# Start of a one-core conv and attention trunk: modulation maps loaded first in a ring, later modulation on half maps

## The chip, the core and the metric

One core of a Trainium2 chip runs the whole program. Its engines are PE (TensorE, matrix multiplies), DVE (VectorE), ACT (ScalarE), POOL (GpSimd) and SP (SyncE, which here only issues transfers). Each engine works through its own list of instructions in order, and waits at an instruction until what it needs is there. The metric is the device time of one execution in microseconds; lower is better.

## What is computed

The reference is a stack of two layers over 1024 latent tokens and 256 context tokens with 1024 features. Layer 0 mixes tokens by a Conformer convolution, layer 1 by attention; both are followed by a SwiGLU network. Every sub-layer is normalized, scaled and shifted by values that come from the conditioning vectors through one linear map per layer:

```python
mod_x = (silu_c @ w_mod[i] + b_mod[i])[:, None, :]
mod_c = silu_cc @ w_mod[i] + b_mod[i]
sh_x, sc_x, g_x, shf_x, scf_x, gf_x = jnp.split(mod_x, N_MOD, axis=-1)
hx = rmsnorm(x, norm_g[i, 0]) * (1.0 + sc_x) + sh_x
hc = rmsnorm(ctx, norm_g[i, 0]) * (1.0 + sc_c) + sh_c
# convolution module of layer 0, on hx and on hc
u = h @ w_pw1 + b_pw1
a, gt = jnp.split(u, 2, axis=-1)
u = a * jax.nn.sigmoid(gt)
u = depthwise_conv(u, w_dw, width=31) + b_dw
u = jax.nn.silu(layernorm(u, ln_g, ln_b))
return u @ w_pw2 + b_pw2
```

So `hx` and `hc` need the first two of the six parts of the modulation (shift and scale), and the rest is needed only behind the convolution.

## The kernel before

Features lie on partitions, in 8 groups of 128; tokens lie along the free dimension, in three pieces: C (256 context tokens), L (the first 512 latent ones) and R (the last 512). Products are made of three matmuls each: a 32-bit operand is split into a rounded part and a remainder (`wh` and `wl` for weights). A weight block of 128x1024 is loaded by SP into one of two buffers `wr`, rounded by ACT (L142), and its remainder is taken by DVE (L146) or POOL (L148).

The beginning, in `build`, has two stages.

In the first, the modulation map is cut into 48 maps of 128 columns (512 KB each). The first 16 (shift and scale) are multiplied on PE by `mod_pe` (L238), two for each of 8 feature groups `k`; their tiles `T_113`, `T_114` and `KB` form a ring of ten buffers. The loop over `k` also moves on the normalizations of C, L and R (`norm_in`): squares on ACT (L383, L386), their sum on DVE (L387), the sum over partitions on PE (L363), the inverse root in small steps on DVE (L368 and L329 to L337), its spread over partitions on PE (L375), and then for each `k` scale on DVE (L395), rounded part on ACT (L400) and remainder on DVE (L401). The rows of C, L and R are loaded by `load_x` into `HR`, `T_106` and `HS`; `cond_row` loads the conditioning vectors as rows (1 MB) for use by DVE.

In the second, `pw1` makes the first projection, block by block (`k` = 0 to 7), each over C, L and R; L457 is its last write for each piece. Copies of its result to the convolution's layout, `split_u` (L157), convolution maps built on DVE (L500, from the tap weights `craw`), convolution matmuls (L526 to L529) and the sum of their halves (L532, L552) run beside it, one convolution step at two of three turns. At each of these turns `modg` may also move on: it is `mod_dve`, which makes maps 16 to 39 of the modulation on DVE, two reductions of 128x1024 for each map (L268), from full maps loaded by SP, one into a tile of `KB` and the next into a weight buffer `wr`, in turn.

What stands where in each engine's list is decided when the program is built: a scheduler takes instructions by the order in which the code issues them, but lets one go ahead where it reckons that its engine would stand idle. Transfers go to the queue of the engine that issues them.

Of the kernel before, what the change touches and what calls it, by code (L numbers as in the profile page):

```python
# [15 lines left out]
P = 128  # L16
# [38 lines left out]
class Kern:  # L55
# [173 lines left out]
    def mod_pe(self, f, raw=None, rows=None):  # L229

        nc = self.nc
        out = self.bank("md")
        if raw is None:
            raw = self.raw()
        nc.sync.dma_start(raw, self.a["wmod"][f])
        with self.later(20):
            for k in range(KT):
                nc.tensor.matmul(out[0:2, 0:P], lhsT=self.cs[:, k, :], rhs=raw[:, k * P:(k + 1) * P],  # L238
                                 start=k == 0, stop=k == KT - 1)
        rows = self.sm(P) if rows is None else rows  # L240
        nc.scalar.copy(rows[0:2, :], out[0:2, 0:P])
        with self.later(40):
            nc.tensor.transpose(out[:, P:P + 2], rows[0:2, :], self.c["ident"][0:2, 0:2])
        for s in range(2):
            nc.scalar.activation(self.mod[0][s][:, f:f + 1], out[:, P + s:P + s + 1], AF.Identity,
                                 bias=self.c["bmod"][:, 0, f:f + 1], scale=1.0)
# [4 lines left out]

    def mod_dve(self, fs, cr, raws, junk):

        nc = self.nc

        def load(i):
            if i >= len(fs):
                return None
            raw = raws[i % len(raws)]
            if raw is None:  # L260
                raw = self.raw()
            nc.sync.dma_start(raw, self.a["wmodT"][0, fs[i]])
            return raw
        nxt = load(0)
        for i, f in enumerate(fs):
            raw, nxt = nxt, load(i + 1)
            for s in range(2):
                nc.vector.tensor_tensor_reduce(out=junk, in0=raw, in1=cr[:, s, :], scale=1.0, scalar=0.0,  # L268
                                               op0=ALU.mult, op1=ALU.add,
                                               accum_out=self.mod[0][s][:, f:f + 1])  # L270
                yield 1.13
        for s in range(2):
            m = self.mod[0][s][:, fs[0]:fs[-1] + 1]
            nc.vector.tensor_tensor(m, m, self.c["bmod"][:, 0, fs[0]:fs[-1] + 1], op=ALU.add)
# [670 lines left out]
    def build(self):  # L945
# [22 lines left out]
        raws = [raws[i][:, j] for j in range(4) for i in range(3) if j < raws[i].shape[1]]  # L968
        for k in range(KT):
            if k == 5:  # L970
                self.pre += [self.wload(a["pw1"][0]), self.wload(a["pw1"][KT])]
            self.mod_pe(k, raws[2 * k % len(raws)])
            self.mod_pe(8 + k, raws[(2 * k + 1) % len(raws)])
# [6 lines left out]
            if k == 1:  # L980
                load_x("L")
                self.cond_row(cr)
                for _ in range(KT + 1):
                    next(gL)
                next(gC)
            if k:
                next(gC)
                next(gL)
            if k == 3:
                xs["R"] = self.T("HS", [P, KT, 512])  # L990
                load_x("R")
                gR = self.norm_in(0, None, (None, "T4", "T5"), *PIECES["R"], hs["R"], xt=xs["R"])
            if k > 3:
                for _ in range(2):
# [24 lines left out]
        modg = self.mod_dve(range(16, 40), cr, (mraw, None), self.ps[:, 5:7].rearrange("p a b -> p (a b)"))  # L1019
# [3 lines left out]
        for k in range(KT):  # L1023
            for i, _ in enumerate(self.pw1(k, hs)):
# [7 lines left out]
                if i % 3 != 2:  # L1032
# [4 lines left out]
        for g0 in (0, CG // 2):  # L1037
            self.split_u(KT - 1, g0, g0 + CG // 2)
        self.derive(0, (1, 2))
# [293 lines left out]
```

## Time and profile before

| | |
|---|---|
| time of three runs | 3049.22, 3055.4, 3057.86 us; median 3055.4 |
| the profiled execution | 3058.17 us, span of its trace 3056.4 us |
| busy share of the span | PE 96%, DVE 62%, ACT 40%, POOL 9% |
| mean granted clock of PE | 0.974 of full speed |

The span runs from the first to the last instruction of the trace; the profiled execution's own time is 1.8 us longer. Shares over the whole span average stages with different limits, so what matters for the beginning is read from windows and from the order of instructions in time.

### The profile page before, as it was taken

Reading aid. Unit: us, or ns where it says so; the run is one execution under the profiler, and the core shown is the slowest. Engines: PE = TensorE matmul, PEld = TensorE weight load, DVE = VectorE, ACT = ScalarE, POOL = GpSimd, SP = SyncE. Lnnn points to the kernel's source line nnn. Section 1 sums busy time; section 2 is a strip of 40 time slices with the busy share of each in tenths; the row PEclk is TensorE's granted clock in tenths of the full one; section 3 lists DMA queues with packets and bytes.
Section 4 is the critical chain, followed back from the end, with each engine's and each line's share of the span. In section 5 each row is a group of like instructions: output and inputs, shape, how many; then the busy total and the mean of one; then the engine's idle time right before and its main releaser. Section 6 shows DMA issues by size and latency. Waiting matters only on the chain. (4 is left out here: it accounts for less than half of the span.)

```text
span 3056.4 us, 39302 instructions
## 1 busy us (share of the span) xinstructions
PE 2927.2 (96%) x15086; PEld 2438.8 (80%) x15086; DVE 1902.2 (62%) x3341; ACT 1207.4 (40%) x1981; POOL 261.1 (9%) x413
## 2 busy tenths in 40 slices
PE   7899969999999999999988999999999999999997
PEld 5788868888888888888877777777787778788886
DVE  5886777866566358333565899766666654743335
ACT  5222255432222234222333688645555542332222
POOL 0000000101112011000013111110000000100000
PEclk9999979999999999999989999989999999999999
DMA  6542424433346235333346311223223132443332
GB/s 236 147 122 75 122 76 138 159 114 126 119 156 198 67 105 157 105 97 97 126 134 151 88 45 47 92 70 90 72 69 86 58 135 95 148 136 97 97 93 66
DMA packets 140716, 336.96 MB, mean 110 GB/s; under 512 B 39920, under 2 KB 61424, under 8 KB 139376
## 3 DMA queue, kind: packets, MB, share of 16 engines
q1 hardware_dynamic: 76432, 221.94, 22.6%
q0 software_dynamic: 37984, 104.42, 11.5%
q10 hardware_dynamic: 26112, 8.10, 1.1%
q8 instruction: 118, 1.93, 0.3%
q14 instruction: 70, 0.57, 0.1%
HBM read 289.76 MB, written 39.19 MB: 108 GB/s over the span
## 5 line engine op out<-in xcount | busy, mean ns | idle before, releaser
L167 PE MATMUL ps<-T,wl 128*128 128x512 f32 (+1 forms) x2128 | 802.9, 378 | 11.8 <-DVE wl L146 11.8
L165 PE MATMUL ps<-T,wh 128*128 128x512 f32 (+1 forms) x2128 | 806.3, 380 | 6.9 <-ACT T L154 4.1
L166 PE MATMUL ps<-T,wh 128*128 128x512 f32 (+1 forms) x2064 | 777.9, 377 | 0.7 <-DVE T L157 0.7
L142 ACT CAST wh<-wr 128x1024 fp32r<-128x1024 f32 x296 | 310.8, 1050 | 796.8 <-PE ps L166 569.0
L146 DVE TENSOR_TENSOR wl<-wr,wh 128x1024 fp32r<-128x1024 f32 x288 | 352.0, 1223 | 311.5 <-ACT wh L142 307.1
L167 PEld LDWEIGHTS ps<-T,wl 128*128 128x128 f32 x2128 | 407.3, 192 | 85.9 <-DVE wl L146 14.1
L165 PEld LDWEIGHTS ps<-T,wh 128*128 128x128 f32 x2128 | 407.2, 192 | 79.7 <-ACT T L154 5.6
L166 PEld LDWEIGHTS ps<-T,wh 128*128 128x128 f32 x2064 | 395.5, 192 | 68.9 <-DVE T L157 2.0
L166 PE MATMUL ps<-HS,wh 128*128 128x512 f32 (+1 forms) x784 | 303.8, 388 | 0.0
L892 DVE TENSOR_TENSOR T<-ps,T 128x512 fp32r<-128x512 f32 x320 | 216.7, 686 | 110.9 <-ACT T L891 109.7
L167 PE MATMUL ps<-HS,wl 128*128 128x512 f32 (+1 forms) x720 | 278.9, 388 | 0.0
L165 PE MATMUL ps<-HS,wh 128*128 128x512 f32 (+1 forms) x720 | 278.7, 389 | 0.0
L891 ACT CAST T<-ps 128x512 fp32r<-128x512 f32 x320 | 185.9, 585 | 194.8 <-PE ps L888 172.8
L888 PE MATMUL ps<-cst,T 128*128 128x128 f32 x1100 | 192.2, 276 | 1.9 <-DVE T L892 1.8
L876 DVE TENSOR_SCALAR_CACHE_REDUCE T<-ps,rq 128x1280 f32<-128x1280 f32 x110 | 169.9, 1544 | 27.8 <-PE ps L870 23.0
L722 DVE TENSOR_TENSOR T<-ps,T 128x512 f32<-128x512 f32 (+1 forms) x168 | 110.3, 662 | 113.1 <-PE ps L167 112.2
L888 PEld LDWEIGHTS ps<-cst,T 128*128 128x128 f32 x1100 | 134.0, 142 | 49.0 <-DVE T L892 28.6
L878 ACT ACTIVATE T<-T,mn 128x1280 f32<-128x1280 f32 x110 | 150.4, 1367 | 57.1 <-DVE T L876 55.2
L166 PEld LDWEIGHTS ps<-HS,wh 128*128 128x128 f32 x784 | 147.5, 188 | 28.6 <-DVE HS L157 0.2
L697 DVE TENSOR_TENSOR sm<-sm,ps 128x256 f32<-128x256 f32 (+1 forms) x88 | 54.5, 619 | 181.4 <-PE ps L167 181.2
L870 PE MATMUL ps<-KB,q 128*128 128x512 f32 (+1 forms) x576 | 146.8, 374 | 14.2 <-DVE HS L876 9.9
L167 PEld LDWEIGHTS ps<-HS,wl 128*128 128x128 f32 x720 | 135.4, 188 | 27.0
(227 smaller groups left out, 4574.0 us busy)
## 6 DMA issues: line engine op xcount, KB each, us to landing
wr<-in_w SPq DMA_DIRECT2D x220, 512.0 KB, 3.5
q<-in_w SPq DMA_DIRECT2D x44, 512.0 KB, 3.5
wr<-in_pw SPq DMA_DIRECT2D x40, 512.0 KB, 3.6
HR<-in_wmodT POOLq DMA_DIRECT2D x56, 256.0 KB, 3.9
q<-in_wmodT POOLq DMA_DIRECT2D x56, 256.0 KB, 3.9
qsd<-T POOLq DMA_DIRECT2D x32, 256.0 KB, 10.7
q<-qsd POOLq DMA_DIRECT2D x32, 256.0 KB, 3.3
wr<-in_wo SPq DMA_DIRECT2D x16, 512.0 KB, 4.4
```

Of the source, the lines that this page charges most:

```text
L142: nc.scalar.copy(hi, raw)
L146: nc.vector.tensor_tensor(lo, raw, hi.bitcast(F32), op=ALU.subtract)
L165: nc.tensor.matmul(out[:, :n], lhsT=wh, rhs=xh, start=k == 0, stop=False)
L166: nc.tensor.matmul(out[:, :n], lhsT=wh, rhs=xl, start=False, stop=False)
L167: nc.tensor.matmul(out[:, :n], lhsT=wl, rhs=xh, start=False, stop=k == nk - 1)
L722: nc.vector.tensor_tensor(yd, out[:, :c1 - c0], yd, op=ALU.add)
L870: nc.tensor.matmul(sc[:, k0:k0 + w], lhsT=q[:, h, :], rhs=kt[:, p * TOK + k0:p * TOK + k0 + w], start=p == 0, stop=p == 1)
L876: nc.vector.tensor_scalar(out=pt, in0=sc, scalar1=rq[:, h:h + 1], scalar2=None, op0=ALU.mult, op1=ALU.min, accum_out=mn)
L878: nc.scalar.activation(pt, pt, AF.Exp, bias=mn, scale=-1.0, accum_out=sums[:, 0, h:h + 1])
L888: nc.tensor.transpose(tp[:, h * P:(h + 1) * P], Ps[h][:, j * P:(j + 1) * P], c["ident"])
L891: nc.scalar.copy(ph, tp)
L892: nc.vector.tensor_tensor(pl, tp, ph.bitcast(F32), op=ALU.subtract)
```

## The change

The first stage loads ahead: ten maps go out before the loop, six of them ahead of L's rows and four behind, and each further map is loaded into a ring buffer when that is free. R's rows are issued at `k` = 3, behind the first two weight blocks of the projection, and the conditioning rows behind R's rows. All weight remainders of the beginning are taken by DVE (`lo_dve`). In the second stage maps 16 to 39 are made by `mod_half`, which stood in the kernel already for later modulation: half maps (128x512) loaded by POOL into three buffers of their own, 96 reductions in place of 48, with a partial sum added at the end. The load of the first tap weights is tied behind R's last remainder by a copy of one column.

```diff
--- before.py
+++ after.py
@@ -226,13 +226,10 @@
         self.col = [[{} for s in range(2)] for l in range(2)]
 
 
-    def mod_pe(self, f, raw=None, rows=None):
+    def mod_pe(self, f, raw, rows=None):
 
         nc = self.nc
         out = self.bank("md")
-        if raw is None:
-            raw = self.raw()
-        nc.sync.dma_start(raw, self.a["wmod"][f])
         with self.later(20):
             for k in range(KT):
                 nc.tensor.matmul(out[0:2, 0:P], lhsT=self.cs[:, k, :], rhs=raw[:, k * P:(k + 1) * P],
@@ -248,30 +245,6 @@
     def cond_row(self, cr):
         self.nc.sync.dma_start(cr.rearrange("p s d -> p (s d)"), self.a["crow"].to_broadcast([P, 2048]))
         self.nc.scalar.activation(cr, cr, AF.Silu)
-
-    def mod_dve(self, fs, cr, raws, junk):
-
-        nc = self.nc
-
-        def load(i):
-            if i >= len(fs):
-                return None
-            raw = raws[i % len(raws)]
-            if raw is None:
-                raw = self.raw()
-            nc.sync.dma_start(raw, self.a["wmodT"][0, fs[i]])
-            return raw
-        nxt = load(0)
-        for i, f in enumerate(fs):
-            raw, nxt = nxt, load(i + 1)
-            for s in range(2):
-                nc.vector.tensor_tensor_reduce(out=junk, in0=raw, in1=cr[:, s, :], scale=1.0, scalar=0.0,
-                                               op0=ALU.mult, op1=ALU.add,
-                                               accum_out=self.mod[0][s][:, f:f + 1])
-                yield 1.13
-        for s in range(2):
-            m = self.mod[0][s][:, fs[0]:fs[-1] + 1]
-            nc.vector.tensor_tensor(m, m, self.c["bmod"][:, 0, fs[0]:fs[-1] + 1], op=ALU.add)
 
     def mod_half(self, l, fs, cr, raws, junk):
 
@@ -966,32 +939,39 @@
             col[("sh", 0)] = self.mod[0][s][:, 0:8]
         raws = [self.T(t, [P, 4, 1024]) for t in ("T4", "T5")] + [self.T("KB", [P, 2, 1024])]
         raws = [raws[i][:, j] for j in range(4) for i in range(3) if j < raws[i].shape[1]]
+
+        def load_map(i):
+            if i < 2 * KT:
+                nc.sync.dma_start(raws[i % len(raws)], a["wmod"][i % 2 * KT + i // 2])
+        for i in range(len(raws)):
+            if i == 6:
+                load_x("L")
+            load_map(i)
+        self.lo_dve = 1.0
         for k in range(KT):
-            if k == 5:
-                self.pre += [self.wload(a["pw1"][0]), self.wload(a["pw1"][KT])]
-            self.mod_pe(k, raws[2 * k % len(raws)])
-            self.mod_pe(8 + k, raws[(2 * k + 1) % len(raws)])
+            for i in (2 * k, 2 * k + 1):
+                self.mod_pe(i % 2 * KT + k, raws[i % len(raws)])
+                load_map(i + len(raws))
             for s in range(2):
                 nc.vector.scalar_tensor_tensor(out=self.col[0][s][0][:, k:k + 1], in0=self.mod[0][s][:, 8 + k:9 + k],
                                                scalar=1.0, in1=c["ng"][:, 0, 0, k:k + 1], op0=ALU.add, op1=ALU.mult)
             if k == 0:
                 for _ in range(KT + 1):
                     next(gC)
-            if k == 1:
-                load_x("L")
-                self.cond_row(cr)
+            if k == 2:
                 for _ in range(KT + 1):
                     next(gL)
-                next(gC)
-            if k:
-                next(gC)
+            next(gC)
+            if k >= 2:
                 next(gL)
             if k == 3:
+                self.pre += [self.wload(a["pw1"][0]), self.wload(a["pw1"][KT])]
                 xs["R"] = self.T("HS", [P, KT, 512])
                 load_x("R")
                 gR = self.norm_in(0, None, (None, "T4", "T5"), *PIECES["R"], hs["R"], xt=xs["R"])
+                self.cond_row(cr)
             if k > 3:
-                for _ in range(2):
+                for _ in range(3 if k < 6 else 2):
                     next(gR)
         for g in (gC, gL, gR):
             for _ in g:
@@ -1016,7 +996,9 @@
         self.cwq, self.cwi = [], 0
         for o, n in ((0, 2), (2 + NC_, 2), (UW - 2, 2)):
             nc.gpsimd.memset(self.U[:, :, o:o + n], 0.0)
-        modg = self.mod_dve(range(16, 40), cr, (mraw, None), self.ps[:, 5:7].rearrange("p a b -> p (a b)"))
+        raws = [mraw[:, :512], mraw[:, 512:], self.sp.tile([P, 512], F32, tag="mr", name="mr", bufs=1)]
+        modg = self.mod_half(0, range(16, 40), cr, raws, self.ps[:, 5, :])
+        nc.vector.tensor_copy(self.craw[:, 0:1], hs["R"][0][1][:, KT - 1, 0:1].bitcast(F32))
         nc.sync.dma_start(self.craw, a["wwin"][0])
         self.conv_maps()
         cg = self.conv()
@@ -1029,13 +1011,15 @@
                     self.more_maps([(cw[:, 2 * j], cw[:, 2 * j + 1]) for j in range(3)])
                 if 12 * k + i >= 22 and i % 3 != 1:
                     next(cg)
-                if i % 3 != 2:
+                for _ in range((1 + (i % 6 == 0)) if k else 0):
                     next(modg, None)
         nc.scalar.activation(self.tiny([P, 16], "nv")[:, :1], c["ones"], AF.Silu)
         for _ in range(4):
             next(cg)
         for g0 in (0, CG // 2):
             self.split_u(KT - 1, g0, g0 + CG // 2)
+        for _ in modg:
+            pass
         self.derive(0, (1, 2))
         for i, _ in enumerate(cg):
             if i in (2, 4):
```

`mod_half`, as it stands in both kernels (`self.tie` is not set yet at this place):

```python
        ahead = len(raws) - 1
        for i in range(ahead):
            load(i)
        for i in range(2 * len(fs)):
            f, h = fs[i // 2], i % 2
            load(i + ahead)
            for s in range(1 if l and f >= 16 else 2):
                nc.vector.tensor_tensor_reduce(out=junk, in0=raws[i % len(raws)], in1=cr[:, s, h * 512:h * 512 + 512],
                                               scale=1.0, scalar=0.0, op0=ALU.mult, op1=ALU.add,
                                               accum_out=(part[:, s] if h else self.mod[l][s])[:, f:f + 1])
                yield 1.0
```

First place: SP's queue from the issue of R's rows on (`HS<-in_xT`). `in_wmod` are maps for PE, `in_wmodT` maps for DVE, `in_pw1` weight blocks, `in_crow` the conditioning rows, `in_wwin` tap weights. Before:

```order
L958 DMA HS_365<-in_xT 128x2x512 x4
L235 DMA T4_113<-in_wmod 128x1024
L235 DMA T5_114<-in_wmod 128x1024
L141 DMA wr1_74<-in_pw1 128x1024
L141 DMA wr0_73<-in_pw1 128x1024
L235 DMA T4_113<-in_wmod 128x1024
L235 DMA T5_114<-in_wmod 128x1024
L235 DMA KB_115<-in_wmod 128x1024
L235 DMA T4_113<-in_wmod 128x1024
L235 DMA T5_114<-in_wmod 128x1024
L235 DMA KB_115<-in_wmod 128x1024
L262 DMA wr1_74<-in_wmodT 128x1024
```

In the changed kernel, from the fifteenth map on:

```order
L945 DMA T5_114<-in_wmod 128x1024
L945 DMA KB_115<-in_wmod 128x1024
L141 DMA wr1_74<-in_pw1 128x1024
L141 DMA wr0_73<-in_pw1 128x1024
L931 DMA HS_377<-in_xT 128x2x512 x4
L246 DMA HR_105<-in_crow 128x2048
L141 DMA wr1_74<-in_pw1 128x1024
L141 DMA wr0_73<-in_pw1 128x1024
L141 DMA wr1_74<-in_pw1 128x1024
L439 DMA KB_619<-HR_105 128x1x32 x4
L1002 DMA KB_619<-in_wwin 128x320
L141 DMA wr0_73<-in_pw1 128x1024
```

R's rows moved behind all maps and two weight blocks, the conditioning rows behind them; no map for DVE stands in this queue any more, and the tap weights stand in front of a weight block.

Second place: DVE at the end of R's inverse root (`nr`, `nq`, `nh`) and the first of R's applies (`sb<-HS`). L500 (before) builds convolution maps `T6`. Before:

```order
L337 SCALAR_TENSOR_TENSOR nr_565<-nq_567,nr_565 128x4
L500 TENSOR_TENSOR T6_621<-q_620,cst_75 128x640
L335 TENSOR_TENSOR nq_567<-nr_565 128x4
L500 TENSOR_TENSOR T6_621<-q_620,cst_75 128x640
L336 TENSOR_TENSOR nq_567<-nq_567,nh_566 128x4
L500 TENSOR_TENSOR T6_621<-q_620,cst_75 128x640
L337 SCALAR_TENSOR_TENSOR nr_565<-nq_567,nr_565 128x4
L335 TENSOR_TENSOR nq_567<-nr_565 128x4
L336 TENSOR_TENSOR nq_567<-nq_567,nh_566 128x4
L337 SCALAR_TENSOR_TENSOR nr_565<-nq_567,nr_565 128x4
L395 SCALAR_TENSOR_TENSOR sb_586<-HS_365,col000_111,ps_72 128x512
L395 SCALAR_TENSOR_TENSOR sb_590<-HS_365,col000_111,ps_72 128x512
```

In the changed kernel, where L430 is the projection's write, L368 and L374 scale and remainder, `T6_106` and `T3` piece L, `HS` and `T5` piece R:

```order
L310 SCALAR_TENSOR_TENSOR nr_557<-nq_559,nr_557 128x4
L430 SCALAR_TENSOR_TENSOR HR_105<-ps_72,cst_75,sm_681 128x256
L368 SCALAR_TENSOR_TENSOR sb_578<-HS_377,col000_111,ps_72 128x512
L368 SCALAR_TENSOR_TENSOR sb_582<-T6_106,col000_111,ps_72 128x512
L368 SCALAR_TENSOR_TENSOR sb_586<-T6_106,col000_111,ps_72 128x512
L374 SCALAR_TENSOR_TENSOR T5_577<-sb_578,mod00_101,T4_576 128x512
L374 SCALAR_TENSOR_TENSOR T3_326<-sb_582,mod00_101,T2_325 128x512
L368 SCALAR_TENSOR_TENSOR sb_590<-HS_377,col000_111,ps_72 128x512
L374 SCALAR_TENSOR_TENSOR T3_326<-sb_586,mod00_101,T2_325 128x512
L368 SCALAR_TENSOR_TENSOR sb_594<-HS_377,col000_111,ps_72 128x512
L374 SCALAR_TENSOR_TENSOR T5_577<-sb_590,mod00_101,T4_576 128x512
L368 SCALAR_TENSOR_TENSOR sb_598<-HS_377,col000_111,ps_72 128x512
```

Convolution maps left this place, and the last applies of piece L and a write of the projection came into it.

Third place: DVE early in block 2, behind the first sums of convolution halves (L532 before, L505 now). Reductions of the modulation are `ISA` rows with `mod00`, `mod01` (streams) or `mpart` (partial sums) as output, each followed by the read of its sum. Before:

```order
L500 TENSOR_TENSOR T6_621<-q_620,cst_75 128x640 x2
L532 TENSOR_TENSOR HR_105<-HR_105,ps_72 128x162
L268 ISA ps_72,mod01_102<-wr0_73,HR_105 128x1024
L268 ISA mod01_102 128x1
L268 ISA ps_72,mod00_101<-KB_619,HR_105 128x1024
L268 ISA mod00_101 128x1
L268 ISA ps_72,mod01_102<-KB_619,HR_105 128x1024
L268 ISA mod01_102 128x1
L157 TENSOR_TENSOR HS_618<-KB_619,HS_618 128x1328
L532 TENSOR_TENSOR HR_105<-HR_105,ps_72 128x162
L457 SCALAR_TENSOR_TENSOR HR_105<-ps_72,cst_75,sm_1111 128x256
L500 TENSOR_TENSOR T6_621<-q_620,cst_75 128x640 x4
```

In the changed kernel:

```order
L505 TENSOR_TENSOR HR_105<-HR_105,ps_72 128x162
L267 ISA ps_72,mpart_824<-KB_619,HR_105 128x512
L267 ISA mpart_824 128x1
L267 ISA ps_72,mod00_101<-mr_625,HR_105 128x512
L267 ISA mod00_101 128x1
L267 ISA ps_72,mod01_102<-mr_625,HR_105 128x512
L267 ISA mod01_102 128x1
L267 ISA ps_72,mpart_824<-KB_619,HR_105 128x512
L267 ISA mpart_824 128x1
L267 ISA ps_72,mpart_824<-KB_619,HR_105 128x512
L267 ISA mpart_824 128x1
L267 ISA ps_72,mod00_101<-KB_619,HR_105 128x512
```

Before, three reductions of full maps and a split of u stood between two sums of halves here; now eight reductions of half maps follow one another, of which six are shown. Over the whole list, 41 of the 48 reductions stood ahead of the last write of block 3 (piece R) before; now all 96 do.

## Rows read from the trace of the kernel before

**Rows 1.** Windows by stage (us, busy us and count, granted clock, DMA share, GB/s).

```profile
9.80:46.00 36.20, 29.61 (x189) 19.55 (x189) 16.93 (x55) 17.73 (x47) 1.97 (x1) 0.86 0.95 369
...
64.00:94.50 30.50, 26.51 (x119) 19.79 (x118) 27.16 (x54) 12.67 (x19) 0.00 (x0) 1.00 0.16 42
94.50:120.00 25.50, 20.06 (x105) 17.04 (x105) 21.97 (x32) 5.50 (x6) 0.00 (x0) 0.93 0.68 202
120.00:361.00 241.00, 239.38 (x1387) 213.44 (x1386) 181.27 (x274) 51.73 (x93) 0.00 (x0) 1.00 0.38 100
...
660.00:680.00 20.00, 20.00 (x112) 17.47 (x111) 17.34 (x41) 7.24 (x18) 3.31 (x7) 1.00 0.50 152
```

**Rows 2.** Timeline of DVE (start, duration, instructions, idle before): sums, R's normalization, first reduction.

```profile
24.14 0.69 DVE L387 TENSOR_TENSOR acc<-acc,sb 128x512 f32<-128x512 f32 x1
...
67.74 0.16 DVE L368 TENSOR_SCALAR nv<-ps 128x4 f32<-128x4 f32 x1 [0.76 <-PE ps L363]
...
76.04 2.06 DVE L395 SCALAR_TENSOR_TENSOR sb<-HS,col,ps 128x512 f32<-128x512 f32 x3 [1.02 <-PE ps L375]
...
86.80 1.23 DVE L268 CUSTOM_DVE_ANT_0 ps<-KB,HR 128x1024 f32<-128x1024 f32 x1
```

**Rows 3.** Timeline of DVE: the projection's last write of blocks 0, 1, 3, 7.

```profile
96.31 0.75 DVE L457 SCALAR_TENSOR_TENSOR HR<-ps,cst,sm 128x512 f32<-128x512 f32 x1
...
133.61 0.74 DVE L457 SCALAR_TENSOR_TENSOR HR<-ps,cst,sm 128x512 f32<-128x512 f32 x1
...
210.17 0.75 DVE L457 SCALAR_TENSOR_TENSOR HR<-ps,cst,sm 128x512 f32<-128x512 f32 x1
...
363.15 0.74 DVE L457 SCALAR_TENSOR_TENSOR HR<-ps,cst,sm 128x512 f32<-128x512 f32 x1
```

**Rows 4.** Timeline of PE: stops at the start of block 1 and in block 4.

```profile
97.19 0.39 PE L448 MATMUL ps<-T,wh 128*128 128x256 f32 x1 [2.66 <-ACT wh L142]
...
225.94 0.50 PE L448 MATMUL ps<-T,wh 128*128 128x512 f32 x1 [1.62 <-DVE HR L457]
```

**Rows 5.** Timeline of PE: modulation maps (L238) and projection matmuls of 256 columns.

```profile
9.79 5.89 PE L238 MATMUL ps<-T,cs 128*2 128x128 f32 x32 [9.79 <-DMA T<-in_wmod]
...
26.68 1.87 PE L238 MATMUL ps<-T,cs 128*2 128x128 f32 x8
...
36.22 3.66 PE L238 MATMUL ps<-T,cs 128*2 128x128 f32 x32
...
40.53 3.65 PE L238 MATMUL ps<-T,cs 128*2 128x128 f32 x32
...
62.63 0.28 PE L448 MATMUL ps<-T,wh 128*128 128x256 f32 x1
62.74 0.28 PE L449 MATMUL ps<-T,wh 128*128 128x256 f32 x1
```

**Rows 6.** DVE by line and shape from 86.8 to 210.2 us (busy, mean ns, idle before).

```profile
L268 DVE CUSTOM_DVE_ANT_0 ps<-KB,HR 128x1024 f32<-128x1024 f32 x21 | 25.8, 1231 | 3.5 <-DMA KB<-in_wmodT 3.1
L500 DVE TENSOR_TENSOR T<-q,cst 128x640 fp32r<-128x640 f32 x32 | 25.7, 819 | 4.1 <-PE ps L527 2.4 <-PE ps L529 1.5
...
L146 DVE TENSOR_TENSOR wl<-wr,wh 128x1024 fp32r<-128x1024 f32 x8 | 9.8, 1223 | 5.1 <-ACT wh L142 5.1
...
L532 DVE TENSOR_TENSOR HR<-HR,ps 128x162 f32<-128x162 f32 x16 | 5.1, 318 | 2.4 <-ACT HR L530 2.4
L157 DVE TENSOR_TENSOR HS<-KB,HS 128x1328 fp32r<-128x1328 f32 x3 | 4.6, 1540 | 2.2 <-ACT HS L154 2.2
```

**Rows 7.** Timeline of DVE: two reductions of a half map, later in the run.

```profile
654.07 0.70 DVE L294 CUSTOM_DVE_ANT_0 ps<-HR 128x512 f32<-128x512 f32 x1 [3.04 <-issue]
...
655.75 0.70 DVE L294 CUSTOM_DVE_ANT_0 ps<-HR 128x512 f32<-128x512 f32 x1
```

**Rows 8.** Landing of half maps by POOL (L286), then of full maps by SP (L262).

```profile
DMA to landing us min/median/max: 2.7/3.9/6.1
...
DMA to landing us min/median/max: 3.4/3.9/6.6
```

## The prediction

> **What bounds the kernel now.** I read the windows by stage first, since a change at the beginning can only pay where PE is not busy [rows 1]: from 9.8 to 46 us PE is busy 29.6 of 36.2 us at a granted clock of 0.86 while the DMA engines are 95% busy; from 64 to 94.5 us it is busy 26.5 of 30.5 us and VectorE 27.2, and from 94.5 to 120 us 20.1 of 25.5 at 0.93. From 120 to 361 us PE misses 1.6 us in 241: there the first projection runs at PE's pace, and VectorE, busy 181 us, has room. So at most some 50 us stand free, all before 120 us.
>
> Next the timeline of VectorE, for marks that both kernels pass. The last normalization (piece R) gets its sums at 67.74, applies scale and shift from 76.04 and ends at 86.80, where the first modulation reduction starts [rows 2]. Then the last write of each block of the projection (piece R, L457): block 0 at 96.31, block 1 at 133.61, block 3 at 210.17, block 7 at 363.15 [rows 3]. I read the time of the change as the shift of the block 7 mark; behind it VectorE's rows for the convolution's end are the same in both orders, and later rows only change places for a few instructions at the start of the attention, which I take as 0 (+-2 us).
>
> **The start.** Modulation maps are multiplied on PE: two maps take 5.89 us at first and 3.66 later, and 0.65 us lies between pairs (36.22 + 3.66 = 39.88 to 40.53) [rows 5]. Before, the last pair was multiplied just ahead of 62 us, because maps were loaded behind rows, and each pair waited for its turn among PE's other work. With all maps ahead in the ring: 9.79 + 5.89 + 7 x (3.66 + 0.65) = 45.9. Stops that stay: piece C's transposes wait for VectorE (0.8); piece L's sums, which ended at 24.83 [rows 2]: L's rows now land behind two more maps (1 MB at the 369 GB/s of [rows 1], 2.8 us), and their squares stand on ScalarE among the copies of more maps, so near 30, when PE comes to them at 28: 2.0; L's transposes behind the root, 1.5; three projection matmuls, 0.6. Last map at 51. From there PE's order puts 39 matmuls of 256 columns (0.115 each, 62.63 to 62.74 in [rows 5]) and 14 of twice the length (0.23) before R's sums: 7.7, and 0.7 + 0.5 for a turn and the sums: R's sums at 60.5, against 67.74.
>
> From sums to first apply was 8.3 us, with six convolution maps between the steps of the root (5 us). Now 12 small steps at 0.2, one weight remainder (1.15) and two applies (1.1), then transposes 0.5: 5 us, first apply at 65.5. But the stretch to the last apply is longer: before it held 16 instructions of 0.67; now four of piece L and one projection write stand among them, 21 x 0.67 = 14.1, and ScalarE's sigmoid of L (0.7) in between holds the last five: 15.5. R ends at **81**, where it was 86.80: 6 us gained. The bounds: 72, if no stop bites (45.9 + 7.7 + 1.2 + 5 + 10.7 = 70.5, and 1.5 for turns), and 86, if PE again falls to the lower clock level, as at 26.68, where eight matmuls took 1.87 us that take 0.9 in the pairs [rows 5].
>
> **The later modulation.** Before: 48 reductions of 128x1024, one per 1.33 us (1.23, and 0.14 for the read of the sum, less overlap), of which 41 stand before the block 3 mark [rows 6]. Now 96 of 128x512. The kernel does the same on half maps later in the run: 0.70 each, and two of them with their reads from 654.07 to 655.75, so 0.84 on average [rows 7]. 96 x 0.84 = 80.6 us instead of 48 x 1.33 = 63.8.
>
> What decides is where they stand. The code hands them out over blocks 1 to 7, but in VectorE's order all 96 come before the block 3 mark. I add up that list, from R's last apply to the mark, each at its duration less the 0.08 by which neighbours overlap: 96 half reductions 80.6; 38 convolution maps x 0.74 = 28.1; 8 weight remainders x 1.14 = 9.1; 7 writes x 0.67 and 3 x 0.40 = 5.9; 3 splits of u x 1.46 and 3 of taps x 0.41 = 5.6; 16 sums of conv halves x 0.24 = 3.8; 2 reductions over channels x 2.47 and 10 small ones = 6.6 [rows 3, 6, 7] (the kinds with fewest pieces are not shown). Sum **140 us**. Before, the same marks lay 123.4 apart (86.80 to 210.17), and VectorE's list for them was 41 x 1.33 + 53 = 108: PE set the pace.
>
> PE's side of that stretch is shorter: from R's end some 7 us to the block 0 mark, block 1 in 30 (37.3 before, less 5.4 of three stops at weights, the longest at 97.19 [rows 4], and 2 of lower clock), blocks 2 and 3 at 37.9 (the mean of blocks 4 to 7, below): 113 us. So VectorE sets the pace in blocks 1 to 3, and PE waits for its maps, weight remainders and freed banks.
>
> **Waits inside that list.** Loads now go through POOL into three buffers, each reloaded when its half is done. Such a load landed in 3.9 us (2.7 to 6.1) [rows 8]; two halves beside it take 3.4. A run of halves with nothing between them then waits 0.7 every third half; I count seven such places in the order, **5 us** (0 at the shortest landing, 20 at 6.1). What is queued behind a late half on VectorE are the writes and maps that PE needs, so these waits count in full.
>
> First the row: from 660 to 680 us VectorE was busy 17.3 of 20 us [rows 1], and in that stretch of the run POOL's loads landed in the 3.9 us above; SP's loads of full maps took 3.9 as well [rows 8]. The Trainium skill ("SBUF — State Buffer", section "SBUF: two separate sides") warns of moving loads this way: descriptors of a DMA issued from GpSimd's queue cannot be written while VectorE runs a two-port operation, and it gives about 0.6 us alone against about 3.1 beside one. By that figure each load would land 2.5 us later, and the seven places would cost 7 x 2.5 = 17 us more, an estimate from that page. The rows do not show it, so the sum goes without.
>
> **Edits at nothing.** The 24 full loads leave SP, which frees it and the two weight buffers: that is what ends the three stops at weights, counted above in PE's side, where VectorE's list hides it. The first two remainders move from POOL to VectorE, counted. The tap load is tied behind R's last piece by a one-column copy (0.2, among the small ones); behind it on SP stands one weight load for block 2, wanted some 30 us later. Two of three table loads on ScalarE go; it is busy 12.7 of 30.5 us there [rows 1].
>
> **Sum.** Block 3 mark at 81 + 140 + 5 = 226, before 210.17. From it to block 7 before: 152.98, of which a stop of 1.6 at 225.94 (a late write behind reductions, [rows 4]) does not return: 151.4, PE's pace. Block 7 at 377.4 against 363.15: **14.2 us later**. The profiled execution took 3058.2 (span 3056.4 and 1.8 around it), 2.8 over the median of the runs; 3055.4 + 14.2 = **3069.6 us**. A difference under 0.3% (9.2 us) is about what a measurement of this kernel cannot tell from none.
>
> **Rivals.**
> (a) No measurable change: R ends at 75 and hardly a load is waited for: 75 + 140 + 1 + 151.4 = 367.4, 3059.7 us. For it: every stop in the start is my estimate. Against: R's rows land near 40 us (14.7 MB up to their end at 369 GB/s), and 140 us stand fixed behind. 0.28.
> (b) Faster: VectorE's list does not bind. Place: blocks 1 to 3. If two half reductions cost hardly more than one full, the gain of the start and of the stops at weights comes through. Break-even is a step of 0.69 us per half reduction (81 + 59.1 + 96p + 5 + 151.4 = 363.15); at 0.60 it is 9 us faster; at 0.50 PE binds, 81 + 113 + 151.4 = 345, that is 3038 us. For it: PE has the work ready. Against: 0.84 is measured. 0.15, most of it for what I have overlooked.
> (c) Loads starve: landing at 6.1 throughout, 15 us more, 3085 us. This is also the case of the rule above. 0.07.
> (d) The start is not earlier at all: R ends at 87 because PE drops to the lower clock: 3075.6 us. The slow matmuls at 26.68 speak for it; denser maps against. 0.05.
> The forecast has 0.45.
>
> **The numbers.** Forecast alone: 3060 to 3080 (R at 78 to 84, waits 0 to 8). The range must leave out at most 2 in 10: from 3050 (which cuts off most of (b)) to 3086 (the long end of (c), both bounds together being unlikely). Slower 0.57 ((c), (d) and the forecast), same 0.28, faster 0.15.
>
> **What would show it.** Right: R's last apply near 81; VectorE without a gap from there to the block 3 mark at about 226, the mark's spacings near 50 us for blocks 2 and 3, and 37 to 38 after; PE idle behind VectorE's maps, writes and remainders in blocks 1 to 3; half reductions at 0.84. Wrong: the block 3 mark before 215, reductions that reach into block 5, or waits for POOL's loads beyond 15 us.

## The result, and the profile after

The changed kernel takes 3065.7 us (median of 5 runs, 3063.3 to 3068.3) against 3052.4 us (5 runs): a ratio of 1.0047 with a 95% interval of 1.0032 to 1.0061, so it is slower by some 14 us (10 to 19). The forecast was 3069.6. The profiled execution of after took 3065.4 us (span 3063.6). Three single executions of the experiments below (one each of before, buf5 and full_own_tie) took over 4200 us, and all medians leave them out.

The windows by stage of after, over the stretches of [rows 1] (us, busy us and count of PE, PEld, DVE, ACT and POOL, granted clock, DMA share, GB/s):

```profile
9.80:46.00 36.20, 33.02 (x256) 23.10 (x256) 19.17 (x63) 16.74 (x54) 0.00 (x0) 1.00 0.97 377
64.00:94.50 30.50, 29.17 (x141) 24.70 (x142) 27.66 (x53) 11.15 (x16) 2.15 (x4) 0.92 0.29 78
94.50:120.00 25.50, 25.03 (x130) 21.39 (x128) 22.55 (x53) 4.98 (x6) 6.44 (x12) 1.00 0.56 169
120.00:361.00 241.00, 225.08 (x1265) 200.59 (x1266) 180.55 (x332) 46.68 (x85) 15.59 (x29) 0.96 0.34 92
```

The three stretches before 120 us, where PE missed 16.0 us in before, now miss 5.0. But from 120 to 361, where it missed 1.6, it now misses 15.9, although VectorE's busy time there is the same to a microsecond. What changed is when that work comes. The three blocks whose list the prediction added up show it (the same columns, after, marks of block 0 to 1, 1 to 2 and 2 to 3):

```profile
89.20:119.80 30.60, 30.33 (x164) 26.20 (x163) 27.65 (x65) 5.46 (x7) 7.52 (x14) 1.00 0.58 169
119.80:171.70 51.90, 40.73 (x224) 35.67 (x224) 47.10 (x103) 8.02 (x15) 9.14 (x17) 0.93 0.48 137
171.70:218.80 47.10, 42.91 (x224) 38.10 (x224) 43.96 (x101) 7.85 (x14) 6.45 (x12) 0.89 0.44 126
```

In block 1 PE hardly stops. In blocks 2 and 3 VectorE is busy for 91 of the 99 us. PE is not its own pace there any more: it misses 15 us, and its clock is below 1.00 as well (0.93 and 0.89).

The timeline of VectorE in after: R's sums, R's first and last apply, the first half reduction, then the last writes of blocks 0 to 3 and 7, which answer to [rows 2, 3] (start, duration, instruction, idle before):

```profile
59.96 0.16 DVE L341 TENSOR_SCALAR nv<-ps 128x4 f32<-128x4 f32 x1 [0.39 <-PE ps L336]
...
65.58 0.75 DVE L368 SCALAR_TENSOR_TENSOR sb<-HS,col,ps 128x512 f32<-128x512 f32 x1 [0.81 <-PE ps L348]
...
80.81 0.74 DVE L374 SCALAR_TENSOR_TENSOR T<-sb,mod,T 128x512 fp32r<-128x512 f32 x1
81.47 0.69 DVE L267 CUSTOM_DVE_ANT_0 ps<-KB,HR 128x512 f32<-128x512 f32 x1
...
89.24 0.75 DVE L430 SCALAR_TENSOR_TENSOR HR<-ps,cst,sm 128x512 f32<-128x512 f32 x1
...
119.76 0.74 DVE L430 SCALAR_TENSOR_TENSOR HR<-ps,cst,sm 128x512 f32<-128x512 f32 x1
...
171.73 0.74 DVE L430 SCALAR_TENSOR_TENSOR HR<-ps,cst,sm 128x512 f32<-128x512 f32 x1
...
218.77 0.74 DVE L430 SCALAR_TENSOR_TENSOR HR<-ps,cst,sm 128x512 f32<-128x512 f32 x1
...
370.30 0.74 DVE L430 SCALAR_TENSOR_TENSOR HR<-ps,cst,sm 128x512 f32<-128x512 f32 x1
```

Block 0's mark is 7.1 us earlier than before, block 1's 13.9 earlier, block 3's 8.6 later and block 7's 7.2 later: a lead of 14 us at block 1, and 22 lost in blocks 2 and 3.

VectorE by line and shape from R's last apply to block 3's mark, after (busy us, mean ns, idle us before), which answers to [rows 6]:

```profile
L267 DVE CUSTOM_DVE_ANT_0 ps<-KB,HR 128x512 f32<-128x512 f32 x64 | 44.7, 698 | 1.8 <-DMA KB<-in_wmodT 0.2
L473 DVE TENSOR_TENSOR T<-q,cst 128x640 fp32r<-128x640 f32 x38 | 30.6, 820 | 0.0
L267 DVE CUSTOM_DVE_ANT_0 ps<-mr,HR 128x512 f32<-128x512 f32 x32 | 22.3, 698 | 1.0 <-DMA mr<-in_wmodT 0.4
```

All 96 half reductions are there (64 + 32). Behind their loads VectorE stood for only 0.6 us (0.2 + 0.4). PE's waits from 82 to 219 us, after (us in total, times, longest):

```profile
PE ps L421 <- DVE HR L430: 14.1, 5, 5.5
PE ps L421 <- ACT sm L429: 0.9, 1, 0.9
```

Of the stops at weights of [rows 4] none is left. PE waits for VectorE's write to free a bank. The late writes show no idle time of VectorE ahead of them (171.73 and 218.77 above): they are queued behind other work, reductions above all.

### The profile page after: what moved, and what is told of

Read it like the earlier page. It is cut to its first block, busy times and chain, and to the rows that moved or that the text cites. A ratio compares the mean times of both kernels' runs of the same rounds, so it can differ in the third digit from the quotient of the medians.

```text
span 3063.6 us, 39483 instructions
## 1 busy us (share of the span) xinstructions
PE 2934.2 (96%) x15086; PEld 2447.9 (80%) x15086; DVE 1912.4 (62%) x3442; ACT 1204.2 (39%) x1979; POOL 281.1 (9%) x459
## 5 line engine op out<-in xcount | busy, mean ns | idle before, releaser
L165 PE MATMUL ps<-T,wh 128*128 128x512 f32 (+1 forms) x2128 | 806.8, 380 | 8.1 <-ACT T L154 4.7
L166 PE MATMUL ps<-T,wh 128*128 128x512 f32 (+1 forms) x2064 | 778.2, 377 | 0.7 <-DVE T L157 0.7
L165 PEld LDWEIGHTS ps<-T,wh 128*128 128x128 f32 x2128 | 407.7, 192 | 80.6 <-ACT T L154 6.2
L421 PE MATMUL ps<-T,wh 128*128 128x512 f32 (+1 forms) x384 | 140.0, 369 | 17.4 <-DVE HR L430 16.4
```

The lines of the kernel that those rows point to most:

```text
L165: nc.tensor.matmul(out[:, :n], lhsT=wh, rhs=xh, start=k == 0, stop=False)
L166: nc.tensor.matmul(out[:, :n], lhsT=wh, rhs=xl, start=False, stop=False)
L421: nc.tensor.matmul(o[:, :n], lhsT=wh, rhs=xh[:, i], start=i == 0, stop=False)
```

## The experiments

Three theories. **A**: the reductions that stand ahead of block 3's mark make VectorE's list the pace of blocks 1 to 3, under which PE's own 38 us per block is the floor. **B**: the half maps' loads (POOL's queue, three buffers) hold VectorE. **C**: the new beginning or its tie costs the time. Every kernel was timed beside before, in four groups of runs, in which before's own median lay between 3052.4 and 3054.4 us; so kernels of different groups are compared by their ratios to before or by block 7's mark. Only the runs called less24, less48 and less48_buf5 leave work out.

**Where the reductions stand (spread).**

```diff
+                self.tie = self.u if k else None
                 for _ in range((1 + (i % 6 == 0)) if k else 0):
                     next(modg, None)
@@ mod_half, load
-                    nc.scalar.copy(raws[i % len(raws)][:, 0:1], self.tie...)
+                    (nc.scalar.copy if l else nc.gpsimd.tensor_copy)(raws[...][:, 0:1], self.tie...)
```

> The kernel after, but each load of a half map is preceded on POOL by a copy of one column of u into the buffer, so that no load, and so no half reduction, can be drawn ahead of the block that hands it out: 14 half reductions stand in each of blocks 1 to 7 in place of 26, 35 and 29 in blocks 1 to 3. Theory A (VectorE's list up to block 3's mark is the pace, and TensorE's 37.9 us per block the floor under it): the list of blocks 1 to 3 is shorter by 46 half reductions or 39 us, TensorE becomes the pace from block 1 on, block 7's mark moves from 370 to 347-352, and the time is 3042-3049 us, faster than before by 3 to 10 us. Theory B (the half maps come late on POOL's queue): the loads start later still, VectorE waits for them, no gain over the kernel after: 3064 us or more. Theory C (the beginning itself or its tie costs the time): nothing changes but the place of the reductions, 3062-3068 us.

Measured: 3059.3 us, 1.0013 (1.0001 to 1.0025): some 10 us below after by the ratios, 7.8 by the mark. The reductions did move: 16, 14, 14, 14, 14, 14 and 4 of them stand in blocks 1 to 7. Blocks 1 to 3 took 26.8, 41.7 and 42.5 us in place of 30.5, 52.0 and 47.0, as A says of the place, but blocks 4 to 6 took 40.6, 40.1 and 43.2 where after has 37.1, 38.2 and 38.1. Block 7's mark is at 362.5, not 350. So the price of the early place is there and the floor was missed: in blocks 3 to 6 PE stood 9.8 us behind the write, with VectorE busy 33 of 42 us. PE's waits from 158 to 336 us:

```profile
PE ps L421 <- DVE HR L430: 9.8, 4, 3.9
```

Enough free time in a block is not enough; what stands directly in front of the write matters. In block 3 all 14 reductions lie between 174.84 and the write at 190.30, the first of them behind a stop of 1.5 us for its load.

**The parts apart (start_full, old_half).** In the first the later modulation is put back together with the places where it is handed out, in the second the beginning.

```diff
-        modg = self.mod_half(0, range(16, 40), cr, raws, self.ps[:, 5, :])
+        modg = self.mod_dve(range(16, 40), cr, (mraw, None), self.ps[:, 5:7]...)
```

> The beginning of the kernel after (ring of maps, R's rows early, tap rows tied) with the later modulation of the kernel before (24 full maps of 128x1024 on SP's queue, in before's buffers). Theory A: R's last apply near 81 in place of 86.8, VectorE's list as before (41 full reductions ahead of block 3's mark), so all later marks and the time move by the 6 us: 3044-3050 us. Theory B gives the same, since there are no half maps. Theory C: the beginning costs, 3056-3066 us.

> The beginning of the kernel before with the later modulation of the kernel after (half maps in three buffers of their own on POOL's queue). Theory A: R ends at 87, 96 half reductions stand ahead of block 3's mark and the list takes about 137 us behind it, mark of block 3 at 224, of block 7 at 376; 3066-3074 us. Theory B: the loads hold it, about the same time, but with stops of VectorE of more than 5 us behind loads. Theory C: 3050-3056 us, no change against before.

Measured: the new beginning alone 3048.1 us, 0.9983 (0.9972 to 0.9995), block 7's mark at 355.8; half maps alone 3072.6 us, 1.0057 (1.0040 to 1.0074), mark at 377.3. The beginning is worth 6 to 7 us with either modulation (377.3 to 370.3, 363.2 to 355.8). C falls. Half maps cost 14 us with either beginning by the marks, and 17 to 20 by the ratios. Over block 2, start_full (windows as above):

```profile
125.20:164.00 38.80, 38.80 (x232) 34.89 (x232) 34.60 (x54) 8.15 (x15) 0.00 (x0) 1.00 0.52 139
```

There VectorE has 34.6 us of work and PE never stops; in after it has 47.1.

**Fewer reductions, same loads (less24, less48).** The condition of less24; less48 has it without `f < 28`.

```diff
+                if l or f < 28 or f >= 40 or s == 0:
                     nc.vector.tensor_tensor_reduce(...)
```

> The kernel after without 24 of the 96 half reductions (stream 1 of the last 12 maps; those columns of the modulation are zero, so that the output is another). The loads are the same. 72 stand ahead of block 3's mark in place of 96. Theory A: block 3's mark comes 24 x 0.84 = 20 us earlier, near 199, block 7's near 350; time 3043-3049 us. Theory B (loads are the pace): the same loads through the same buffers, the mark moves by 0-5 us, 3060-3066 us. Theory C: no change.

> The kernel after without all of stream 1's 48 half reductions of the 24 later maps (those columns of the modulation are zero, so that the output is another); the 48 loads are the same. Now 5, 20, 23 and 0 half reductions stand in blocks 0 to 3 in place of 6, 26, 35 and 29. Theory A with the floor that the run with 24 left out showed (38.1 us from mark to mark from block 2 on, about 27 for block 1): block 1 gives back 4 us, block 2 12 x 0.84 = 10, block 3 9; block 7's mark near 348, 3043-3050 us. Theory B (the loads of half maps are the pace): the marks stay within 5 us of the kernel after, 3060 us or more.

Measured: 3056.7 us (1.0007, 0.9995 to 1.0018) and 3057.4 us (1.0017, 1.0004 to 1.0030); block 7's mark at 362.7 and 365.1. Both missed A's number. With 24 left out, block 3 fell from 47.0 to 38.5, onto the floor, but block 2 stayed at 51.8 though five reductions fewer stand in it: VectorE's busy time there fell by 3.2 us, and its stops behind loads grew from 0.2 to 3.1. With 48 left out, block 1 even grew (34.2) and block 2 took 49.9 with 23 reductions in place of 35. VectorE's waits in less48 from block 0's to block 2's mark say why:

```profile
DVE ps L271 <- DMA KB<-in_wmodT: 9.0, 10, 2.2
DVE ps L271 <- DMA mr<-in_wmodT: 7.3, 9, 1.8
```

16.3 us behind loads, against under 1 in after. With one reduction per half in place of two, a buffer is free sooner but its next load takes as long (medians of 3.2 and 3.3 us by buffer from 90 to 180 us). B is wrong of after and right in part of this kernel: the loads are a second pace close behind the list.

**More buffers (buf5, less48_buf5).**

```diff
+        raws += [self.acc(512), self.acc(512)]
```

> The kernel after with five buffers for the half maps in place of three (the two more are the tiles acc, which nothing else uses in these blocks); VectorE's order is the same (6, 26, 35 and 29 half reductions in blocks 0 to 3). Theory A (with all 96 reductions VectorE's list is the pace; the profile after shows under 1 us of stops behind loads): nothing to gain, 3061-3069 us, block 7's mark within 3 us of 370. Theory B (the loads hold VectorE, hidden in the profile): faster by 5 us or more.

> The kernel without stream 1's 48 half reductions (another output) with five buffers: 5, 27 and 16 half reductions in blocks 0 to 2. In the run with three buffers VectorE stood behind loads for 10 us in block 1 and 8 us in block 2, since each load had only one reduction to hide it. If that is why the time did not fall as far as the list is shorter: these stops fall under 4 us together, blocks 1 and 2 take 28-31 and 38-42 us, block 7's mark is at 347-354, the time 3042-3052 us. If the list is not the pace at all (against theory A): block 2 stays near 50 us and the time at 3055 us or more.

Measured: with all reductions 3063.8 us, 1.0034 (1.0021 to 1.0047), mark of block 7 at 371.1, no stop behind a load from 81 to 219 us: nothing gained by the mark, as A says, and the interval overlaps after's. With 48 left out 3051.7 us, 0.9988 (0.9973 to 1.0003), mark at 355.6: 9.5 us earlier by two buffers and the order that comes with them. VectorE's waits over blocks 1 and 2 in that kernel:

```profile
DVE HS L157 <- ACT HS L154: 6.3, 2, 3.5
DVE ps L271 <- DMA KB<-in_wmodT: 2.8, 4, 1.5
...
DVE ps L271 <- DMA acc<-in_wmodT: 1.4, 2, 0.7
DVE ps L271 <- DMA mr<-in_wmodT: 0.2, 1, 0.2
```

4.4 us behind loads, a little over the 4 expected; block 2 took 40.1 us, block 3 37.9. Block 1 stayed at 34.9 with 27 reductions in it, which the expectation had at 28 to 31, and the mark missed 347 to 354.

**Halving apart from the buffers (full_split, full_own).** The first cuts each full reduction in two but keeps before's buffers; the second keeps buffers of its own but reduces whole maps.

```diff
+                for h in range(2):
                     nc.vector.tensor_tensor_reduce(out=junk[:, :512], in0=raw[:, h * 512:h * 512 + 512], ...)
@@ full_own
+        modg = self.mod_dve(range(16, 40), cr, (mraw, self.acct), ...)   # loads on POOL
```

> The beginning of after with before's full maps, their buffers and SP's queue, as in the run with the full maps, but each full reduction made as two half reductions (96 of 0.84 us in place of 48 of 1.37), so that halving is priced without the buffers of its own. Blocks 0 to 4 hold 7, 37, 21, 16 and 15 halves; with full maps they held 7, 15, 11, 8 and 7. Theory A, halving is a small part and the early place of the work is the large one: block 1's VectorE work grows from 30.6 to about 41 us and its spacing from 36.6 to 41-45, the later blocks stay under the 38-39 us of TensorE; 3051-3058 us. Rival, halving alone costs what the later modulation costs: 96 x 0.84 - 48 x 1.37 = 15 us in full, 3062-3066 us.

> The beginning of after; the later maps are loaded and reduced whole (48 reductions of 1.37 us) but in two buffers of their own on POOL's queue (the second is the two tiles acc as one), so that only the halving is undone and the buffers of their own stay: 4, 14, 19 and 11 full reductions in blocks 0 to 3, all ahead of block 3's mark. Theory A: VectorE's work of block 2 is 47 - 35 x 0.84 + 19 x 1.37 = 44 us, of block 3 44 - 29 x 0.84 + 11 x 1.37 = 35 us; spacings 28-30, 45-49 and 38 us, block 7's mark at 355-360, 3049-3057 us. Rival, it is the halving and nothing else: as fast as the run with before's full maps or faster, 3042-3048 us. Rival, it is the early place and nothing else: 3062 us or more.

Measured: 3053.7 us (1.0003, 0.9990 to 1.0016) and 3059.8 us (1.0016, 1.0004 to 1.0028). With start_full and after they make a square, all with the new beginning (ratio to before; block 7's mark):

| | before's buffers | buffers of their own, on POOL's queue |
|---|---|---|
| full reductions | 0.9983; 355.8 | 1.0016; 367.3 |
| half reductions | 1.0003; 357.0 | 1.0047; 370.3 |

Halving costs 6 and 9 us by the ratios (1 and 3 by the marks), buffers of their own 10 and 13 us (12 and 13 by the marks). Before's ring takes every other buffer from the weights' two, so a map can't be loaded before a weight buffer is free; that this held the reductions back is read from their places. Freed of that, they are drawn ahead: full_own has 19 in block 2 where start_full has 11, its VectorE is busy 46.1 us there and the block takes 51.3, more than the 45 to 49 expected; time and mark, too, lie above the 3049 to 3057 and 355 to 360 of theory A. In full_split the longer reductions hold a weight buffer instead: PE waits 8.7 us for a weight in block 1. The right column also loads on POOL, and full_own hands out 7 reductions a block from block 1 on, in place of 8 from block 0 on; these were not tried apart from the buffers.

**Spread in three groups, and without the tie (spread3, notie).**

```diff
+                self.tie = self.u[:, (CTX + 512, 0, CTX)[i // 4]:] if k else None
@@ notie
-        nc.vector.tensor_copy(self.craw[:, 0:1], hs["R"][0][1][:, KT - 1, 0:1].bitcast(F32))
```

> As the run with the spread reductions (each load behind a copy on POOL), but the copied column is that of the piece of u that was written last (R of the block before, C, L in turn), so that the loads of a block start in three groups and not in one behind piece C. Theory A, the 9.8 us that TensorE stood behind the last write in blocks 3 to 6 came from reductions bunched in front of it: the spacings of blocks 2 to 6 fall from 40-43 to 38-40, block 7's mark to 352-357, 3046-3054 us. Rival, the stops come from the load that is waited for in VectorE's order, and they only change place: 3056-3062 us.

> The kernel after without the copy of one column that ties the tap rows' load behind R's last apply. Theory A: the list of VectorE ahead of block 3's mark is as long (96 half reductions), only its order near block 0 changes; 3062-3069 us. Theory C (the tie holds the maps of the convolution and with them block 1): faster than after by 5 us or more, 3058 us or less.

Measured: spread3 3069.5 us, 1.0056 (1.0040 to 1.0073), block 7's mark at 374.1: no faster than after, and slower than the expectation and its rival had it. Its blocks 2 to 6 took 43.3 to 44.1 us. VectorE's waits in it from 158 to 336 us:

```profile
DVE ps L267 <- DMA KB<-in_wmodT: 23.9, 8, 4.2
DVE ps L267 <- DMA mr<-in_wmodT: 9.2, 3, 4.1
```

33 us behind loads, where spread has 6.9: the order puts the reductions where the tie allows the load, and VectorE waits up to 4.2 us for it. A tie that releases a load just ahead of its use turns the landing into a stop. The tap rows' tie costs nothing: without it 3064.4 us, 1.0041 (1.0025 to 1.0057), block 7's mark at 369.6.

**Tied full maps (full_own_tie).** The same copy on POOL ahead of each full map's load.

```diff
+            if self.tie is not None:
+                nc.gpsimd.tensor_copy(raw[:, 0:1], self.tie[:, 0:1].bitcast(F32))
             nc.gpsimd.dma_start(raw, self.a["wmodT"][0, fs[i]])
```

> As the run before with full maps in buffers of their own, but each load stands behind a copy on POOL of one column of u, so that 6 or 8 full reductions stand in each of blocks 1 to 6 (4, 6, 8, 6, 8, 6, 8, 2). VectorE has 22.3 + 8 x 1.37 = 33 us of work per block, under TensorE's 38.1. Theory A with loads hidden by the second buffer: 38-40 us per block, block 7's mark at 348-356, 3041-3050 us, the fastest of these kernels. Rival, as with the spread half maps: tied loads start together behind the write of piece C, VectorE's order bunches the reductions and waits for the loads in it, 41-43 us per block, block 7's mark near 362 and 3056-3062 us.

Measured: 3046.0 us, 0.9980 (0.9968 to 0.9992), the best median here; by the tie alone it lies 11 us below full_own by the ratios and 8.2 by the mark. It beats both kernels; from start_full (3048.1) it can't be told. But block 7's mark is at 359.2, later than expected and than start_full's. Windows over blocks 2 to 4:

```profile
114.70:158.40 43.70, 39.74 (x226) 35.29 (x226) 32.18 (x50) 8.07 (x15) 4.34 (x8) 0.96 0.39 106
158.40:197.30 38.90, 38.90 (x231) 34.84 (x230) 30.06 (x47) 8.15 (x15) 3.16 (x6) 1.00 0.41 107
197.30:240.00 42.70, 39.34 (x221) 34.81 (x221) 32.54 (x51) 8.50 (x16) 4.35 (x8) 0.96 0.40 109
```

The block with 6 reductions runs at PE's pace; each of those with 8 takes 4 to 5 us more, with a stop of PE behind the write, though VectorE is busy only 32 of 43 us. Block 2, VectorE ahead of its first reduction and PE behind the write:

```profile
133.98 1.23 DVE L270 CUSTOM_DVE_ANT_0 ps<-acc,HR 128x1024 f32<-128x1024 f32 x1 [3.88 <-DMA acc<-in_wmodT]
```

```profile
149.23 0.80 PE L450 MATMUL ps<-T,wh 128*128 128x512 f32 x1 [3.96 <-DVE HR L459]
...
150.25 0.63 PE L452 MATMUL ps<-T,wl 128*128 128x512 f32 x1
150.68 0.63 PE L450 MATMUL ps<-T,wh 128*128 128x512 f32 x1
...
153.20 0.39 PE L452 MATMUL ps<-T,wl 128*128 128x512 f32 x1
153.43 0.39 PE L450 MATMUL ps<-T,wh 128*128 128x512 f32 x1
```

VectorE waits 3.9 us for the first load, and all 8 reductions then stand between 133.98 and the write at 148.43 that PE waits for. So in the blocks with 8 the rival's mechanism holds (loads that start together, bunched reductions, 41 to 43 us), although the time is that of theory A.

## Why the prediction was right, step by step

- **The start.** Right: sums at 59.96 (60.5 forecast), first apply at 65.58 (65.5), R's last apply ends at 81.5 (81). Two sums on the way are slips: the terms written down give 59.7 for R's sums, not 60.5, and 14.8 from first to last apply, not 15.5; the latter took 15.9, since VectorE stood 1.9 us behind ScalarE's rounding (L373) and not 0.7. The lower clock did come, from about 62 to 69 us (granted 0.50 from 64 to 68, the lower of the two levels, 1.2 GHz), where matmuls of 512 columns lie 0.43 us apart that lie 0.23 apart later. PE in after:

```profile
66.62 0.63 PE L421 MATMUL ps<-T,wh 128*128 128x512 f32 x1
67.05 0.63 PE L422 MATMUL ps<-T,wh 128*128 128x512 f32 x1
...
70.58 0.39 PE L423 MATMUL ps<-T,wl 128*128 128x512 f32 x1
70.80 0.40 PE L422 MATMUL ps<-T,wh 128*128 128x512 f32 x1
```

It set in behind R's sums' matmuls, after a stretch (60 to 62 us) in which PE was busy for 1.3 of 2 us, and left the first apply where it was forecast. Rival (d) did not happen; start_full shows the 6 to 7 us of the beginning by themselves.
- **The list and its waits.** "VectorE sets the pace in blocks 1 to 3" holds for blocks 2 and 3; block 1 kept to PE's pace (30.5 us, VectorE busy 27.6). The spacings of 52.0 and 47.0 us are near the 50 forecast, and PE stopped for banks, but not for maps and weight remainders as forecast. buf5 excludes the loads; full_own_tie against full_own shows that the place of the reductions alone is worth 8 us by the mark and 11 by the ratios. Of the sum of 140 + 5, the stretch from 81.47 to 218.77 took 137.3 with all waits in it. Three things differ. "Waits inside that list" was 5 us and measured 0.6. VectorE also waited 6.3 + 1.7 us for ScalarE there (ahead of the splits of u and of the sums), which was not in the sum. VectorE's waits from 81.4 to 219.5 us:

```profile
DVE HS L157 <- ACT HS L154: 6.3, 3, 2.5
DVE HR L505 <- ACT HR L503: 1.7, 2, 1.3
```

So the instructions themselves fill 129 us and not 140, and nearly all of that miss is one term, the half reduction at 0.84 us. From start to start (timeline of VectorE in after), 62 of the 96 take 0.79, those that another reduction follows; 34 take 0.63, those that another kind of instruction follows, which starts together with the read of the sum:

```profile
88.63 0.70 DVE L267 CUSTOM_DVE_ANT_0 ps<-mr,HR 128x512 f32<-128x512 f32 x1
89.24 0.15 DVE L267 DVE_READ_ACCUMULATOR2_ANT mod<- 128x1 f32 x1
89.24 0.75 DVE L430 SCALAR_TENSOR_TENSOR HR<-ps,cst,sm 128x512 f32<-128x512 f32 x1
...
101.01 0.70 DVE L267 CUSTOM_DVE_ANT_0 ps<-KB,HR 128x512 f32<-128x512 f32 x1
...
101.80 0.70 DVE L267 CUSTOM_DVE_ANT_0 ps<-KB,HR 128x512 f32<-128x512 f32 x1
```

Together they take 70.3 us where the sum had 80.6; the rest of the list took 58.5 where it had 59. The mean of 0.73 is close to the break-even of 0.69 that rival (b) named: by the prediction's own formula it makes after only 4 us slower. The ScalarE waits, which the sum left out, brought back most of what the reductions fell short.

- **The rule on POOL's loads.** In blocks 1 to 3 VectorE was busy 119 of 130 us and POOL's loads still landed in 3.2 and 2.9 us by buffer (medians from 90 to 180 us; 2.7 to 5.5 over the whole run). The Trainium skill ("SBUF — State Buffer", section "SBUF: two separate sides") gives its figure for VectorE operations in a two-port mode, and says further down that `tensor_tensor` has no such mode. VectorE's work here is nearly all of that kind (products and sums of two tensors), so by that rule the 17 us did not apply, and no run here tests the rule itself. Rival (c) did not happen in after.
- **Behind block 3.** 151.5 us to block 7's mark (151.4 forecast).
- **The sum.** Block 7's mark moved by 7.2 us, not 14.2: 7.7 us were too many in the list with its waits, 0.5 too few in R's end. The forecast time stood on 3055.4, the median of three runs, where five gave 3052.4. The spans differ by the same 7.2, which lies below the interval of the timed runs (10 to 19). That the medians differ by 13.3, close to the forecast, is not shown by the two traces: before's profiled execution is at the upper end of its runs (3058.2 against a median of 3052.4), after's is at its median. Single executions do differ that much behind block 7's mark: span less mark is 2686.9 us in buf5's trace and 2699.4 in less48's. But chance may not be all of it: median less mark lies at 2687 to 2692 us for the four kernels with full reductions and at 2692 to 2697 for the ten with halves. What makes that difference stays open, since only one execution of a kernel has a trace. The good fit of the time is therefore in part luck; by the traces the change costs half of the forecast.

## What to carry to other kernels

An in-order engine with free time in a stage can still set its pace: sum its list between two marks that another engine waits for, and look at what stands directly ahead of the write. Buffers of their own take away a brake as well as a wait; if shared buffers had kept filler work back, the scheduler may draw it all ahead, so tie it to the stage it belongs to, early enough for its loads to land; no tie here got that quite right. When a resource is cut, ask which pace lies next: leaving out half of the reductions here brought out the loads, which had cost 0.6 us. And price a short instruction by its step in the order in which it will stand, not by its step in a run of its kind.

## What the runs showed of the hardware

- The time of one and the same kernel goes with the granted clock: over 29 runs of before (3045 to 3061 us) each 0.001 less of mean granted clock goes with 2 us more, with a correlation of -0.8 (1.7 us in two more groups, of 23 and 34 runs). Which is the cause was not tried. So kernels that differ by 3 us can't be ranked by a handful of runs.
- A stop of 3 to 4 us of PE behind a write went with a lower granted clock in that block: 0.96 in both blocks of full_own_tie with such a stop, 1.00 in the one between. Right behind the stop of 3.96 us the granted clock was 0.50 (149.8 to 151.9 us), the lower level of 1.2 GHz, and 0.98 from 152 to 156.
- A multiply-reduce with a sum is two instructions on VectorE, and the second, the read of the sum, costs nothing where another kind of instruction follows: half reductions took 0.63 us from start to start there and 0.79 in a run of them (34 and 62 cases in after). Full ones took 1.16 and 1.32 in full_own (28 and 19 cases), so halving raised the price of the same sums by a fifth.
